# Keeping the second part of every mix, cross and up weight tile in DRAM after the first pass

## The chip, the cores and the metric

The kernel runs on one core of a Trainium2 chip. The metric is device time in microseconds of one execution. Three runs of the kernel before gave 1808.7, 1804.29 and 1805.51 us, a median of 1805.51. The profiled execution took 1804.14 us; its trace spans 1802.0 us, so 2.1 us lie outside the span.

## What is computed

One layer of an encoder runs over 1024 prompt frames and 32 sample frames with shared weights. The part that the change touches is the second half of the layer, cut to its core here:

```
bo = (cb * conv) @ w_conv_out
x  = x + (sigmoid(ga) * a + sigmoid(gb) * bo) @ w_mix_out
hc = rms_norm(x, g_cross)
cq = hc @ w_cq
s  = einsum(cq, mem_k) * MEM_SCALE ;  p = softmax(s)
x  = x + einsum(p, mem_v) @ w_co
hm = rms_norm(x, g_mlp)
x  = x + square(relu(hm @ w_up)) @ w_down
```

The model width is 1024, the hidden width 4096, the cross-attention has 4 heads of 64 over 256 memory tokens. All inputs and outputs are float32.

## The kernel before

**Two parts for each operand.** Each matrix product is made of three TensorE products in a rounded float32 format. A helper, `split`, makes the two parts of an operand: ScalarE copies the value into the rounded format (`hi`), and VectorE subtracts `hi` from the value (`lo`). `gemm` then adds up, for each block of 128 rows, `hi*hi`, `hi*lo` and `lo*hi` (lines 183, 184 and 185), the last one with the weight's `lo` tile, which the code calls `wl`.

**The weight stream.** A weight tile has 128 partitions of 1024 numbers (512 KB). The list `worder` holds the tiles in the order of their use, and `next_w` keeps two tiles ahead of the one in use (`LOOK = 2`). `issue_w` prepares one tile: SyncE's queue loads the raw tile into one of two `wr` buffers (line 145), ScalarE casts it into one of three `wh` buffers and VectorE subtracts into one of three `wl` buffers (lines 125 and 126 inside `split`). A raw buffer is free again when both have read it. A `wh` or `wl` buffer is free when the products with the tile three places earlier are done.

**Three passes over the same weights.** The frames are cut into three chunks of 384, 384 and 288 columns (chunks 0, 1 and 2; the last one holds the sample frames too). The products with `w_conv_out` (8 tiles), `w_mix` (8), `w_cq` (2), `w_co` (2) and the first 8 tiles of `w_up` are made chunk by chunk, so each of these tiles is prepared three times. One tile then serves one product of 24 matmuls.

**Kept second parts.** The dictionary `kept` names tiles whose `wl` is stored in DRAM when it is first made (line 162, right behind the subtraction). In the passes for the chunks 1 and 2 such a tile's `wl` is loaded (line 156), and ScalarE alone casts `wh` (line 157). Before the change `kept` holds the tiles with odd numbers: 4 of `w_conv_out`, 4 of `w_mix`, 1 of `w_cq`, 1 of `w_co` and 4 of the first 8 of `w_up`, 14 in all, hence 14 stores and 28 loads.

**The order around them.** `trunk(c)` is the list of conv_out products and mix products of chunk c. `do_conv_out` loads a partial result (line 1026), `do_mix` loads a slice of x (line 1041), adds it to the product (line 1045), and forms two parts of the scaled sum for the cross-attention (lines 262 and 263). `cross_steps(c)` is the cross-attention of chunk c: query products, scores, turns, values (lines 1156 to 1171) and the output product `do_co` (lines 1183 to 1185, its sum at 1187). `beside` interleaves the cross steps of a chunk with the products of the next one: cross 0 beside trunk 1, cross 1 beside trunk 2, cross 2 beside the up products of the chunks 0 and 1. `normed_split` (lines 1212 to 1216) prepares the MLP's input of the chunks 0 and 1. After these come the up products of chunk 2, together with `combine` (lines 1261 to 1273), which prepares sums and differences for the later up tiles, and then those tiles themselves.

**What decides the order of instructions.** The code gives a program order; a scheduler moves instructions within each engine's stream by its own estimates of time, except those inside `pin`. Each engine runs its stream in order. All DMAs named here, loads, stores and weights, are issued on SyncE's queue in its stream order: one that waits for its data or its buffer holds back all behind it. Product sums lie in three PSUM banks (`acc`); a bank is free when VectorE has read it.

Of the kernel before, what the change touches and what calls it, by code (L numbers as in the profile page):

```python
# [10 lines left out]
F32 = mybir.dt.float32  # L11
# [27 lines left out]
def hybrid_step(ctx: ExitStack, tc: tile.TileContext, io):  # L39
    nc = tc.nc  # L40
    act, dve, pool_e, pe, sp = nc.scalar, nc.vector, nc.gpsimd, nc.tensor, nc.sync
# [3 lines left out]
    def nm(s):  # L45
        uid[0] += 1
        return f"{s}_{uid[0]}"
# [64 lines left out]
    plan, worder, kept = [], [], {}  # L112
# [11 lines left out]
    def split(hi, lo, src):  # L124
        act.copy(hi, src)  # L125
        dve.tensor_sub(lo, src, hi.bitcast(F32))  # L126
# [15 lines left out]
    def fetch_w():  # L142
        raw = wp.tile([P, 1024], F32, tag="wr", bufs=2, name=nm("wr"))
        src = weight(worder[wpos[0] + len(fetched)])
        sp.dma_start(raw.rearrange("p (i c) -> p i c", i=4) if len(src.shape) == 3 else raw, src)
        fetched.append(raw)

    def issue_w():
        if not fetched:
            fetch_w()  # L150
        raw = fetched.pop(0)
        key = worder[wpos[0]]
        hi = wp.tile([P, 1024], F32R, tag="wh", name=nm("wh"))
        lo = wp.tile([P, 1024], F32R, tag="wl", name=nm("wl"))
        if kept.get(key) is not None:
            sp.dma_start(lo.bitcast(F32), kept[key])
            act.copy(hi, raw)
        else:
            split(hi, lo, raw)
            if key in kept:  # L160
                kept[key] = dram.tile([P, 1024], F32, name=nm("wl_d"))
                sp.dma_start(kept[key], lo.bitcast(F32))
        ready.append((worder[wpos[0]], (hi, lo)))
        wpos[0] += 1

    def next_w(key):
        while len(ready) <= LOOK and wpos[0] < len(worder) and worder[wpos[0]] is not STOP:
            issue_w()
        k, w = ready.pop(0)
        assert k == key, (k, key)  # L170
        return w
# [106 lines left out]
    def norm_x():  # L278
# [37 lines left out]
        with tc.manual_schedule(engines={mybir.EngineType.Activation, mybir.EngineType.DVE}):  # L316
            parts(0, range(2))
            issue_w()
            parts(0, range(2, NF))
            issue_w()  # L320
            issue_w()
            squares(0)
# [115 lines left out]
    def do_K(pr, extras=()):  # L438
        def fn(w):
            kt = at_tile([P, NT], F32, "kt")  # L440
            ktt[pr] = kt
            for c, (o, n) in enumerate(CH):
                a = acc_tile([P, n])
                gemm(a, w, xg[c])
                dve.tensor_mul(kt[:, o : o + n], a, R[c])
                after(extras, c)
            sp.dma_start(io["o_k"][pr], kt[:, 896:])

        return fn
# [22 lines left out]
    def do_Q(kv, j, extras=()):  # L472
        def fn(w):
            for c, (o, n) in enumerate(CH):
                npr = min(n, NPR - o)
                if j == 0:
                    qs[kv, c] = at_tile([P, 4, npr], F32R, "QA" if c < 2 else "QB", 2 if c < 2 else 1)
                    if n > npr:
                        qs[kv, 3] = at_tile([P, 4, n - npr], F32R, "QC")
                a = acc_tile([P, n])  # L480
                gemm(a, w, xg[c])
                t = tmp(n)
                dve.scalar_tensor_tensor(t, a, 0.125, R[c], op0=ALU.mult, op1=ALU.mult)
                parts = [(qs[kv, c], slice(0, npr))]
                if n > npr:
                    parts.append((qs[kv, 3], slice(npr, n)))
                for q, s in parts:
                    for e in range(2):
                        own, other = slice(64 * e, 64 * e + 64), slice(64 - 64 * e, 128 - 64 * e)
                        h = 2 * j + e  # L490
                        act.copy(q[own, h], t[own, s])
                        dve.tensor_sub(q[other, h], t[own, s], q[own, h].bitcast(F32))
                after(extras, c)

        return fn
# [156 lines left out]
    def do_gate(to, extras=()):  # L652
        def fn(w):
            for c, (o, n) in enumerate(CH):
                a = acc_tile([P, n])
                gemm(a, w, xg[c])
                t = gate_slot(c, 0)
                dve.tensor_mul(t, a, R[c])
                act.activation(t, t, AF.Sigmoid)
                to(c, t)  # L660
                after(extras, c)

        return fn
# [59 lines left out]
    for i, h in enumerate(hosts):  # L723
# [16 lines left out]
        if h[0] == "Q":  # L740
            fn, key = do_Q(h[1], h[2], extras), qt(h[1], h[2])
        elif h[0] == "K":
            fn, key = do_K(h[1], extras), ("w_in", 8 + h[1])
        elif h[0] == "G":
            fn, key = do_gate(lambda c, t: sa.__setitem__((c, 0), t), extras), ("w_in", 34)
        else:
            fn, key = do_conv(*h, extras), conv_w(h[1], h[0])
# [743 lines left out]

    up0 = lambda c: [do_up(j, c) for j in range(NF)]
    for name, n in (("w_conv_out", NF), ("w_mix", NF), ("w_cq", 2), ("w_co", 2), ("w_up", NF)):
        kept.update(((name, j), None) for j in range(1, n, 2))

    left = beside([], trunk(0), [(i, lambda: pump(2)) for i in range(NF)])
    item(lambda: pump(0))
# [343 lines left out]
```

## Time and profile before

| | |
|---|---|
| runs | 1808.7, 1804.29, 1805.51 us (median 1805.51) |
| profiled execution | 1804.14 us |
| its span in the trace | 1802.0 us |
| mean granted TensorE clock | 0.991 |
| DVE busy over the span | 1172.4 us (65%) |
| ACT busy over the span | 797.2 us (44%) |
| HBM read and written | 242.62 MB and 86.67 MB |
| stores of `wl` (line 162) | 14, from 802.5 to 1092.4 us |
| loads of `wl` (line 156) | 28, from 869.2 to 1173.3 us |

In the rows of the trace, PE is TensorE's matmuls, PEld its weight loads, DVE is VectorE, ACT ScalarE, POOL GpSimd and SP SyncE, whose DMA queue is SPq. L126 is line 126 of the kernel. In a view of windows, each engine has its busy time in the stretch and its number of instructions, then come the clock that TensorE was granted, the busy share of the 16 DMA engines and the GB/s that they moved. In a view of waits, a row names who waited, for whom, the total in us, the number of times and the longest. In a timeline, a row has start and duration in us, engine, line, operation and tiles; a bracket holds the idle time ahead of it and what ended it. Matmuls are pipelined, so their rows overlap; the distance of the starts is what one costs.

### The profile page before, as it was taken

The numbers are of one execution on the slowest core, as the hardware profiler recorded it, in microseconds if no ns is written. First come the engines' busy times: TensorE is split into PE (matmuls) and PEld (weight loads), VectorE is DVE, ScalarE is ACT, GpSimd is POOL, SyncE is SP. The second block draws the span as 40 slices with busy tenths as digits, with TensorE's granted clock in tenths as the row PEclk, the third lists the DMA queues.
The fourth block names the chain that finished last, engine by engine and source line by source line (L and its number), as shares of the span: only waits on it lengthen the run. The fifth ranks groups of instructions, "written<-read, shape, count | busy, mean of one in ns | idle before, by whom it ended". The sixth has DMA issues, their size and how long they took to land. (4 is left out here: it accounts for less than half of the span.)

```text
span 1802.0 us, 30258 instructions
## 1 busy us (share of the span) xinstructions
PE 1756.7 (97%) x11110; PEld 1736.2 (96%) x11110; DVE 1172.4 (65%) x2164; ACT 797.2 (44%) x1566; POOL 593.8 (33%) x681
## 2 busy tenths in 40 slices
PE   8999999999999999999999999999999899999998
PEld 7999999999999999999999989999999899999997
DVE  6776767868665646647566867776666566436673
ACT  8643535435344334335565745632222334324453
POOL 0013245653454444502224242385555300100101
PEclk9999999999999999999999989999999999999999
DMA  5332234344346888758755656744433577436573
GB/s 180 100 112 92 87 109 147 118 151 143 127 150 237 308 288 276 262 200 274 256 194 205 231 204 233 260 151 152 141 122 131 172 243 240 161 126 205 195 248 125
DMA packets 184002, 331.27 MB, mean 184 GB/s; under 512 B 18784, under 2 KB 139648, under 8 KB 183728
## 3 DMA queue, kind: packets, MB, share of 16 engines
q1 hardware_dynamic: 170080, 280.95, 46.6%
q0 software_dynamic: 13776, 48.41, 7.6%
q8 instruction: 87, 1.43, 0.3%
q14 instruction: 59, 0.48, 0.1%
HBM read 242.62 MB, written 86.67 MB: 183 GB/s over the span
## 5 line engine op out<-in xcount | busy, mean ns | idle before, releaser
L125 ACT CAST wh<-wr 128x1024 fp32r<-128x1024 f32 x224 | 235.3, 1050 | 405.4 <-PE acc L184 106.2
L126 DVE TENSOR_TENSOR wl<-wr,wh 128x1024 fp32r<-128x1024 f32 x224 | 298.0, 1330 | 169.8 <-ACT wh L125 158.4
L183 PE MATMUL acc<-X,wh 128*128 128x384 f32 (+1 forms) x864 | 282.1, 327 | 8.4 <-ACT wh L125 8.4
L184 PE MATMUL acc<-X,wh 128*128 128x384 f32 (+1 forms) x864 | 279.4, 323 | 0.0
L185 PE MATMUL acc<-X,wl 128*128 128x384 f32 (+1 forms) x864 | 278.7, 323 | 0.2 <-DVE wl L126 0.2
L183 PE MATMUL acc<-Y,wh 128*128 128x384 f32 (+1 forms) x624 | 202.2, 325 | 3.7 <-ACT Y L762 2.2
L184 PE MATMUL acc<-Y,wh 128*128 128x384 f32 (+1 forms) x624 | 201.7, 324 | 0.3 <-DVE Y L763 0.3
L185 PE MATMUL acc<-Y,wl 128*128 128x384 f32 (+1 forms) x624 | 201.8, 324 | 0.0
L259 POOL TENSOR_TENSOR xacc<-xacc,ct 128x384 f32<-128x384 f32 (+1 forms) x62 | 74.7, 1206 | 339.3 <-ACT ct L257 337.5
L183 PEld LDWEIGHTS acc<-X,wh 128*128 128x128 f32 x864 | 163.0, 189 | 9.0 <-ACT wh L125 8.4
L184 PEld LDWEIGHTS acc<-X,wh 128*128 128x128 f32 x864 | 163.4, 189 | 0.6
L185 PEld LDWEIGHTS acc<-X,wl 128*128 128x128 f32 x864 | 163.1, 189 | 0.8 <-DVE wl L126 0.8
L183 PEld LDWEIGHTS acc<-Y,wh 128*128 128x128 f32 x624 | 117.4, 189 | 5.1 <-ACT Y L762 2.8
L184 PEld LDWEIGHTS acc<-Y,wh 128*128 128x128 f32 x624 | 117.5, 188 | 0.9 <-DVE Y L763 0.9
L185 PEld LDWEIGHTS acc<-Y,wl 128*128 128x128 f32 x624 | 117.5, 189 | 0.0
L1587 PE MATMUL acc<-Y,wh 128*128 128x384 f32 (+1 forms) x352 | 113.6, 323 | 0.7 <-DVE lt L1378 0.7
L1588 PE MATMUL acc<-Y,wh 128*128 128x384 f32 (+1 forms) x352 | 113.6, 323 | 0.0
L1589 PE MATMUL acc<-Y,wl 128*128 128x384 f32 (+1 forms) x352 | 113.3, 322 | 0.0
L125 ACT CAST PTh<-pt 128x512 fp32r<-128x512 f32 (+3 forms) x94 | 46.2, 517 | 116.4 <-PE pt L572 108.2
L851 PE MATMUL acc<-Y,wh 128*128 128x384 f32 x248 | 84.0, 339 | 1.7 <-ACT s L1335 0.9
L707 POOL TENSOR_TENSOR ws<-ws 128x256 f32<-128x256 f32 x92 | 82.8, 899 | 5.2
L1244 POOL TENSOR_TENSOR ct<-ct 128x288 f32<-128x288 f32 (+1 forms) x48 | 45.1, 941 | 119.0 <-DVE ct L1240 45.6
(360 smaller groups left out, 4767.8 us busy)
## 6 DMA issues: line engine op xcount, KB each, us to landing
wr<-in_w_in SPq DMA_DIRECT2D x52, 512.0 KB, 3.4
wr<-in_w_up SPq DMA_DIRECT2D x48, 512.0 KB, 3.8
wr<-in_w_down SPq DMA_DIRECT2D x32, 512.0 KB, 3.8
wr<-wsum_d SPq DMA_DIRECT2D x32, 512.0 KB, 3.6
wl<-wl_d SPq DMA_DIRECT2D x28, 512.0 KB, 4.2
wr<-in_w_conv_out SPq DMA_DIRECT2D x24, 512.0 KB, 4.5
wr<-in_w_mix SPq DMA_DIRECT2D x24, 512.0 KB, 4.3
ct<-b_d SPq DMA_DIRECT2D x48, 192.0 KB, 3.9
```

The costliest lines, as they stand in the source:

```text
L125: act.copy(hi, src)
L126: dve.tensor_sub(lo, src, hi.bitcast(F32))
L183: pe.matmul(out, wh[:, a], hi, start=(k == 0), stop=False)
L184: pe.matmul(out, wh[:, a], lo, start=False, stop=False)
L185: pe.matmul(out, wl[:, a], hi, start=False, stop=(k == len(acts) - 1))
L259: pool_e.tensor_tensor(acc, acc, sq, op=ALU.add)
L707: pin(pool_e.tensor_tensor(t[:, to], t[:, x], t[:, y], op=ALU.add))
L851: pe.matmul(acc, wh[:, a], hi, start=(start and k == 0), stop=False, skip_group_check=True)
L1244: pool_e.tensor_tensor(h, t, t, op=ALU.mult)
L1587: pe.matmul(a, wh[:, s], hi, start=(start and k == 0), stop=False, skip_group_check=True)
L1588: pe.matmul(a, wh[:, s], lo, start=False, stop=False, skip_group_check=True)
L1589: pe.matmul(a, wl[:, s], hi, start=False, stop=(stop and k == len(acts) - 1), skip_group_check=True)
```

## The change

Two things are changed. The store of a kept `wl` is no longer issued right behind its subtraction but is put on a list, `parts_out`, and issued at the beginning of the next `issue_w`. And `kept` holds all tiles of `w_mix`, `w_cq`, `w_co` and the first 8 of `w_up`, while of `w_conv_out` it holds the odd ones as before: 24 tiles, hence 24 stores and 48 loads.

```diff
+    parts_out = []
+
     def issue_w():
+        for to, lo in parts_out:
+            sp.dma_start(to, lo.bitcast(F32))
+        parts_out.clear()
         if not fetched:
             fetch_w()
         raw = fetched.pop(0)
@@
             split(hi, lo, raw)
             if key in kept:
                 kept[key] = dram.tile([P, 1024], F32, name=nm("wl_d"))
-                sp.dma_start(kept[key], lo.bitcast(F32))
+                parts_out.append((kept[key], lo))
         ready.append((worder[wpos[0]], (hi, lo)))
         wpos[0] += 1
@@
     for name, n in (("w_conv_out", NF), ("w_mix", NF), ("w_cq", 2), ("w_co", 2), ("w_up", NF)):
-        kept.update(((name, j), None) for j in range(1, n, 2))
+        kept.update(((name, j), None) for j in range(n) if j % 2 or name != "w_conv_out")
```

## The prediction

> **What bounds the kernel now.** I read the page first, then the stretch from 800 to 1190 us stage by stage, because all stores and loads of `wl` lie there (802.5 to 1173.3 us), then who TensorE waits for in it, and last the timelines around the waits.
>
> ```profile
> span 1802.0 us, 30258 instructions
> PE 1756.7 (97%) x11110; PEld 1736.2 (96%) x11110; DVE 1172.4 (65%) x2164; ACT 797.2 (44%) x1566; POOL 593.8 (33%) x681
> ...
> L126 DVE TENSOR_TENSOR wl<-wr,wh 128x1024 fp32r<-128x1024 f32 x224 | 298.0, 1330 | 169.8 <-ACT wh L125 158.4
> ```
>
> TensorE is the bound: 1802.0 - 1756.7 = 45.3 us idle in the whole kernel. The change adds and removes no matmul, so it can gain only idle TensorE time and time at a reduced clock. A subtraction of a weight tile takes 1.33 us of VectorE, which has 35% of the span to spare, so its busy time as such is worth nothing; only where it stands ahead of something that TensorE waits for does it count.
>
> ```profile
> core 0: us, PE busy (x) PEld busy (x) DVE busy (x) ACT busy (x) POOL busy (x), PEclk, DMA share, GB/s
> 800.00:880.00 80.00, 77.66 (x443) 76.24 (x442) 54.78 (x83) 42.16 (x72) 15.86 (x13) 1.00 0.82 280
> 880.00:960.00 80.00, 79.82 (x475) 79.12 (x474) 51.17 (x92) 46.44 (x88) 26.13 (x22) 1.00 0.60 203
> 960.00:1050.00 90.00, 83.36 (x552) 79.89 (x551) 64.73 (x125) 55.58 (x110) 27.94 (x28) 0.94 0.63 213
> 1050.00:1140.00 90.00, 87.81 (x553) 86.45 (x552) 65.11 (x125) 49.41 (x105) 22.54 (x22) 1.00 0.65 223
> 1140.00:1190.00 50.00, 46.98 (x329) 46.12 (x328) 39.43 (x56) 27.81 (x47) 34.53 (x29) 1.00 0.79 275
> ```
>
> The rows are, from the top: trunk 0; cross 0 beside trunk 1; cross 1 beside trunk 2; cross 2 beside the up products of the chunks 0 and 1; the up products of chunk 2. TensorE's idle time in them is 2.3, 0.2, 6.6, 2.2 and 3.0 us, 14.4 in all. The third row holds almost half of it, has the busiest VectorE of the first four and is the only one with a clock below 1.00.
>
> ```profile
> PE acc L1183 <- DVE Gb L1045: 2.8, 3, 1.5
> PE acc L1183 <- DVE Ga L1187: 1.5, 3, 0.9
> PE acc L1183 <- ACT Y L1165: 1.3, 2, 0.9
> PE acc L183 <- DVE ct L1240: 1.3, 1, 1.3
> PE o L1156 <- DVE tO L1159: 1.2, 1, 1.2
> ```
>
> These are TensorE's five longest waits from 860 to 1190 us. Four of them are for VectorE; none is for a load of `wl`, though 28 of them stand in the stretch.
>
> **What the removed subtractions are worth.** The change removes 20 subtractions, 2 for each of the 10 newly kept tiles, 20 x 1.33 = 26.6 us of VectorE. The comparison of the two instruction orders agrees: VectorE has 20 rows fewer (1955 to 1935). Three of the removed ones stand at stalls.
>
> ```profile
> 1026.49 1.21 DVE L126 TENSOR_TENSOR wl<-wr,wh 128x1024 fp32r<-128x1024 f32 x1
> ...
> 1028.09 0.54 DVE L1159 TENSOR_TENSOR tO<-o,tO 64x384 f32<-64x384 f32 x1
> ...
> 1030.79 1.21 DVE L126 TENSOR_TENSOR wl<-wr,wh 128x1024 fp32r<-128x1024 f32 x1
> ...
> 1033.90 0.44 DVE L1045 TENSOR_TENSOR Gb<-acc,ct 128x288 f32<-128x288 f32 x1
> ```
>
> ```profile
> 1028.68 0.45 PE L1156 MATMUL o<-PTh,mv 128*128 128x384 f32 x1 [1.15 <-DVE tO L1159]
> ...
> 1034.39 0.45 PE L1183 MATMUL acc<-Y,wh 128*128 128x384 f32 x1 [1.45 <-DVE Gb L1045]
> 1034.68 0.34 PE L1184 MATMUL acc<-Y,wh 128*128 128x384 f32 x1
> 1034.85 0.33 PE L1185 MATMUL acc<-Y,wl 128*128 128x384 f32 x1
> 1035.59 0.44 PE L1183 MATMUL acc<-Y,wh 128*128 128x384 f32 x1 [0.40 <-ACT Y L1165]
> 1036.71 0.44 PE L1184 MATMUL acc<-Y,wh 128*128 128x384 f32 x1 [0.68 <-DVE Y L1171]
> ...
> 1038.26 0.69 PE L1183 MATMUL acc<-Y,wh 128*128 128x384 f32 x1 [0.93 <-DVE Ga L1187]
> 1038.74 0.52 PE L1184 MATMUL acc<-Y,wh 128*128 128x384 f32 x1
> 1039.06 0.52 PE L1185 MATMUL acc<-Y,wl 128*128 128x384 f32 x1
> ```
>
> VectorE runs without a gap from the first subtraction to the add at 1033.90. The sum at 1028.09, which ends TensorE's wait of 1.15 us, comes 1.2 us earlier without it; the add that ends the wait of 1.45 us comes up to 2.4 us earlier without both. In the changed kernel's order neither stands there any more. Both waits go: 2.6 us. The later waits (0.40, 0.68, 0.93) are turns between ScalarE, VectorE and TensorE on the last head; I leave them in.
>
> **The clock.** Starts of neighbouring matmuls are 0.17 us apart at 1034.68 and 0.32 us apart at 1038.74.
>
> ```profile
> 1038.00:1048.00 10.00, 8.38 (x26) 7.37 (x27) 6.86 (x13) 5.08 (x10) 4.88 (x6) 0.51 0.32 98
> ```
>
> Just behind the series of waits the granted clock falls to 0.51 for 10 us. TensorE is busy for 8.38 us of it, so about 8.38 x 0.49 = 4.1 us are lost. The series from 1027.5 to 1038.3 holds 1.15 + 1.45 + 0.40 + 0.68 + 0.93 = 4.6 us of idle time; without the first two 2.0 are left. I take it that the clock then stays up, and count 4.1 us; the bounds are 0 and 4.1.
>
> The Trainium skill's page "TensorE: Matmul & The Clock Gate", section "What's actually happening", says that the clock falls to half after at least one idle window of about 3.4 us. No single wait here is longer than 1.45 us, so by that sentence the waits would not be the cause, removing two of them would not bring the clock back, and the sum would lack this term. The trace has the fall right behind them, and I go by the trace.
>
> **The stall in chunk 2's up products.**
>
> ```profile
> 1161.34 1.05 ACT L125 CAST wh<-wr 128x1024 fp32r<-128x1024 f32 x1 [3.18 <-DMA wr<-in_w_up]
> 1162.42 1.23 DVE L126 TENSOR_TENSOR wl<-wr,wh 128x1024 fp32r<-128x1024 f32 x1 [3.92 <-ACT wh L125]
> 1163.56 0.45 DVE L1240 SCALAR_TENSOR_TENSOR ct<-acc,R 128x288 f32<-128x288 f32 x1
> 1164.06 0.40 PE L183 MATMUL acc<-Y,wh 128*128 128x288 f32 x1 [1.27 <-DVE ct L1240]
> 1164.30 0.29 PE L184 MATMUL acc<-Y,wh 128*128 128x288 f32 x1
> 1164.43 0.30 PE L185 MATMUL acc<-Y,wl 128*128 128x288 f32 x1
> ```
>
> Here VectorE's stream stood for 3.92 us at a subtraction whose raw tile came late, and the eviction behind it, which frees TensorE's bank, had to wait though it needed neither. The subtraction of this tile (an even one of `w_up`) is removed: 1.3 us gained, the late raw tile being then ScalarE's matter alone.
>
> **What is added.** 10 stores and 20 loads of 512 KB, 15.7 MB, all on SP's queue.
>
> ```profile
> L156 SPq DMA_DIRECT2D wl<-wl_d x28: 319/326/656, 869.2 to 1173.3; - x28
> ...
> DMA to landing us min/median/max: 3.5/4.2/6.0
> ```
>
> ```profile
> SPq L156 <- PE acc L185: 34.3, 18, 4.0
> ```
>
> A load waits on SP until the products of the tile three places earlier have freed its buffer, and SP stands meanwhile for 34.3 / 18 = 1.9 us on the mean. Behind it are the slices of x (line 1041), the stores of normed rows and the raw tiles. From the freed buffer, two products are left until the tile is needed: 2 x 24 matmuls at 0.17 us in the chunks 0 and 1, 8.2 us, and at 0.13 us in chunk 2 (the starts at 1164.30 and 1164.43), 6.2 us. The median load is there after 0.33 + 4.2 = 4.5 us, the slowest after 6.3. All 28 loads of before cost TensorE nothing, so I count the 20 new ones at 0; the bounds are 0 and the second rival's price below.
>
> The stores of `w_mix` fall into the first stage, which runs at 280 GB/s and 0.82 of the DMA engines. There the 4 new ones add 2.1 MB, 26 GB/s over 80 us, and the share goes to about 0.90. Weight tiles are short there at one place:
>
> ```profile
> PE acc L183 <- ACT wh L125: 1.6, 1, 1.6
> ```
>
> I count this wait once more, 1.6 us; the bounds are 0 and once for each of the 4 stores, 6.4 us. The other 6 stores (2 of cross weights, 4 of `w_up`) go where the share is 0.60 to 0.65 and I count them at 0. That a store is issued one tile late changes next to nothing: in both orders it stands just ahead of the raw load of the tile two places on, and both wait for the same subtraction. Its cover is that shared wait; without it a store would cost SP its 0.33 us of issue.
>
> **The sum.** -2.6 - 4.1 - 1.3 + 1.6 = -6.4 us. Against the profiled execution that is 1804.1 - 6.4 = 1797.7. That execution lies 1.4 us below the median of the runs shown, so for a run I say 1799.
>
> **The rivals.**
>
> *The clock falls all the same.* The remaining waits of 2.0 us within 4 us, or a new order around them, could bring it down again. For this speaks that 0.93 us of them directly precede the slow matmul at 1038.26. Then the sum is -2.3 and the time about 1803. It is also the result by the page's sentence on the idle window.
>
> *The loads of `wl` land late* (slower). The place is the up products, from 1100 to 1185 us, where in both passes every tile now needs one.
>
> ```profile
> 1140.00:1150.00 10.00, 10.00 (x64) 9.83 (x63) 7.85 (x14) 7.52 (x16) 5.41 (x6) 1.00 0.98 372
> ```
>
> The DMA engines are already full there for 10 us, and 4 more loads fall into the last stage alone. The mechanism decides from the point where a load takes over 6.2 us from freed buffer to landing. If it takes twice the median, 0.33 + 8.4 = 8.7 us, two tiles need 8.7 instead of 6.2, 1.25 us more a tile, 10 us over 8 tiles. With the gains above but for the stall at 1164, which would then only move, that is 1805.5 - 2.6 - 4.1 + 1.6 + 10 = 1810. Against it: the slowest of 28 loads took 6.0 us.
>
> *More than the three stalls goes.* If all idle time from 960 to 1050 us went as well as the slow clock, it would be 6.6 + 4.1 + 1.3 - 1.6 = 10.4 us, 1795. Against it: part of that waiting is for slices of x, which now stand behind more waiting loads on SP.
>
> ```profile
> DVE Gb L1045 <- DMA ct<-in_x: 5.2, 2, 3.1
> ```
>
> *The change does not do what it says.* The instruction order shows the 20 subtractions gone and the 30 DMAs there, so I give this nothing.
>
> **How the numbers follow.** The forecast has 0.42, its own range 1797 to 1802; the clock that falls all the same 0.27, 1800 to 1806; late loads 0.21, 1806 to 1816; more than the stalls 0.10, 1792 to 1797. A change of under 0.3%, 5.4 us, cannot be told from none by runs that spread over 4.4 us; so faster means below 1800.1, slower above 1810.9. Below 1800.1 lie most of the forecast (0.33), the last case (0.10) and a little of the second (0.02): 0.45. Above 1810.9 I put three quarters of the late loads, 0.16, and 0.04 for places that I have not priced: 0.20. The rest, 0.35, is within. The range 1793 to 1812 leaves out the far ends of the two outer cases.
>
> **What would show it.** In the profile after: no wait over 0.5 us for lines 1159 and 1045 near 1030 us, a clock of 1.00 from 1030 to 1050 us, and no stall at the first evictions of chunk 2's up products. Wrong would be a granted clock near 0.5 in that stage as before, waits of line 185 for a DMA `wl<-wl_d`, landings above 6.2 us there, or longer waits for weight casts in the mix products of chunk 0.

## The result and the profile after

The changed kernel takes 1811.64 us (median of 21 runs, 1807.22 to 1814.47), the kernel before in the same comparison 1805.5 us (21 runs). The ratio is 1.0032, 95% interval 1.0023 to 1.0041: 0.32% or about 6 us slower, where 6.4 us less were forecast. The profiled execution is a short one, 1807.3 us with a span of 1805.5 us; two more executions of the same kernel that were traced later have spans of 1808.4 and 1807.6 us. The trace shown is therefore read for where time goes, and the medians for how much it is.

The head of the page after, and the row of the weight subtractions in its costliest groups:

```profile
span 1805.5 us, 30279 instructions
...
PE 1756.0 (97%) x11110; PEld 1736.4 (96%) x11110; DVE 1143.3 (63%) x2144; ACT 796.3 (44%) x1566; POOL 574.9 (32%) x681
...
L126 DVE TENSOR_TENSOR wl<-wr,wh 128x1024 fp32r<-128x1024 f32 x204 | 268.3, 1316 | 153.2 <-ACT wh L125 152.5
```

The 20 subtractions are gone and VectorE is busy for 29 us less, yet TensorE's idle time has risen from 45.3 to 49.5 us (1805.5 - 1756.0). The five stages, in the view of windows (span of the window, busy time and instructions of PE, PEld, DVE, ACT and POOL, granted clock, DMA share, GB/s):

```profile
800.00:880.00 80.00, 77.09 (x430) 75.52 (x429) 51.66 (x78) 39.69 (x69) 14.90 (x13) 0.98 0.86 294
880.00:960.00 80.00, 80.00 (x479) 79.89 (x478) 50.73 (x93) 47.61 (x91) 23.48 (x22) 1.00 0.74 246
960.00:1050.00 90.00, 79.88 (x539) 76.98 (x538) 53.52 (x115) 53.81 (x105) 21.49 (x24) 0.97 0.72 247
1050.00:1140.00 90.00, 89.11 (x560) 88.75 (x559) 57.36 (x120) 50.35 (x108) 25.95 (x25) 0.99 0.81 275
1140.00:1190.00 50.00, 47.40 (x322) 46.38 (x321) 31.04 (x53) 27.22 (x47) 28.48 (x29) 0.97 0.93 337
```

TensorE's idle time, before and after: 2.3 and 2.9; 0.2 and 0.0; 6.6 and 10.1; 2.2 and 0.9; 3.0 and 2.6 us. The time that the clock costs (PE busy times one less the granted clock) has to be added. It is 5.0 us in the third row before and 0 in the others; after, it is 1.5, 0, 2.4, 0.9 and 1.4 us. Both together rose by 2.1, -0.2, 0.9, -0.4 and 1.0 us, which makes 3.4 of the 3.5 us between the two spans. So in these two traces the first and the last row lose as much as the third; what belongs to the change and what to the single execution, the runs below have to tell.

Idle time alone rose most in the third row. VectorE lost 11 us of work there (64.7 to 53.5), and TensorE idles 3.5 us more. That speaks against VectorE's load of work as what TensorE waits for there. The longest waits of TensorE from 860 to 1190 us (who waited, for whom: total us, times, longest):

```profile
PE acc L188 <- DVE Ga L1050: 4.5, 2, 2.7
PE acc L1188 <- DVE Gb L1050: 4.0, 3, 2.6
PE acc L188 <- ACT wh L162: 1.8, 1, 1.8
PE acc L1188 <- DVE Ga L1192: 1.6, 1, 1.6
PE acc L190 <- DMA wl<-wl_d: 0.7, 1, 0.7
```

The wait for `tO` (1.2 us before) is gone. In first place stand two rows for line 1050, the add of x to the mix product, which was line 1045 and cost 2.8 us before. What VectorE itself waits for, from 1000 to 1060 us:

```profile
DVE Gb L1050 <- DMA ct<-in_x: 3.5, 2, 2.7
DVE Ga L1050 <- DMA ct<-in_x: 3.5, 2, 2.9
```

The adds wait for their slices of x. That is not new: before, VectorE waited for slices of x for 6.3 us in this window (5.2 for `Gb`, 1.1 for `Ga`). What is new is that TensorE waits with it, 8.5 us in place of 2.8. One of the adds, on VectorE and then on TensorE (a bracket holds the idle time ahead and what ended it):

```profile
1028.52 0.46 DVE L1050 TENSOR_TENSOR Ga<-acc,ct 128x288 f32<-128x288 f32 x1 [2.87 <-DMA ct<-in_x]
```

```profile
1029.03 0.40 PE L188 MATMUL acc<-M,wh 128*128 128x288 f32 x1 [1.80 <-DVE Ga L1050]
...
1035.98 0.40 PE L188 MATMUL acc<-M,wh 128*128 128x288 f32 x1 [2.67 <-DVE Ga L1050]
...
1046.82 0.69 PE L1188 MATMUL acc<-Y,wh 128*128 128x384 f32 x1 [2.56 <-DVE Gb L1050]
```

The slice was issued on SyncE's queue at 1020.60, 7.9 us ahead of the add:

```profile
1018.19 0.88 SPq L161 DMA_DIRECT2D wl<-wl_d  x2
1019.27 0.33 SPq L145 DMA_DIRECT2D wr<-in_w_mix  x1
1020.21 0.33 SPq L145 DMA_DIRECT2D wr<-in_w_co  x1
1020.60 0.45 SPq L1046 DMA_DIRECT2D ct<-in_x  x1
...
1023.85 0.38 SPq L161 DMA_DIRECT2D wl<-wl_d  x1
1027.99 0.33 SPq L145 DMA_DIRECT2D wr<-in_w_mix  x1
1028.42 0.38 SPq L161 DMA_DIRECT2D wl<-wl_d  x1
1029.28 0.33 SPq L145 DMA_DIRECT2D wr<-in_w_co  x1
1029.66 0.42 SPq L1046 DMA_DIRECT2D ct<-in_x  x1
```

Two `wl` tiles and two raw tiles, 2.1 MB, were issued in the 2.4 us ahead of a slice of 147 KB. At 372 GB/s, the rate of the fullest window quoted in the prediction, these take 5.6 us by this estimate. The next slice shows a second effect: it is issued only at 1029.66, behind four weight loads, the second of which started 4.1 us after the first (1023.85 and 1027.99). The landing times of the 8 slices of this pass, in the view of line 1046 from 1000 to 1060 us:

```profile
DMA to landing us min/median/max: 3.8/5.3/7.9
```

Before, in the view of line 1041:

```profile
DMA to landing us min/median/max: 3.2/3.8/5.5
```

From here two theories were tried against each other:

- *Slices of x.* The new loads of `wl` cost little by landing late themselves. They hold back the small loads of x behind them on SyncE's queue in the third pass, and the VectorE add of x then holds TensorE's bank.
- *Spread or other.* The loss comes from the stores, from the late store, from late `wl` tiles, or is spread over all stages as DMA traffic.

### The profile page after: what moved, and what is told of

It is laid out like the page before. It is cut to its first block, busy times and chain, and to the rows that moved or that the text cites. A ratio compares the mean times of both kernels' runs of the same rounds, so it can differ in the third digit from the quotient of the medians.

```text
span 1805.5 us, 30279 instructions
## 1 busy us (share of the span) xinstructions
PE 1756.0 (97%) x11110; PEld 1736.4 (96%) x11110; DVE 1143.3 (63%) x2144; ACT 796.3 (44%) x1566; POOL 574.9 (32%) x681
## 5 line engine op out<-in xcount | busy, mean ns | idle before, releaser
L125 ACT CAST wh<-wr 128x1024 fp32r<-128x1024 f32 x204 | 214.2, 1050 | 386.2 <-PE acc L189 82.5
L126 DVE TENSOR_TENSOR wl<-wr,wh 128x1024 fp32r<-128x1024 f32 x204 | 268.3, 1316 | 153.2 <-ACT wh L125 152.5
L264 POOL TENSOR_TENSOR xacc<-xacc,ct 128x384 f32<-128x384 f32 (+1 forms) x62 | 70.4, 1137 | 347.6 <-ACT ct L262 345.1
L857 PE MATMUL acc<-Y,wh 128*128 128x384 f32 x248 | 83.3, 336 | 0.0
L856 PE MATMUL acc<-Y,wh 128*128 128x384 f32 x248 | 83.2, 336 | 0.0
```

The lines of the kernel that those rows point to most:

```text
L264: pool_e.tensor_tensor(acc, acc, sq, op=ALU.add)
L856: pe.matmul(acc, wh[:, a], hi, start=(start and k == 0), stop=False, skip_group_check=True)
L857: pe.matmul(acc, wh[:, a], lo, start=False, stop=False, skip_group_check=True)
```

## The experiments

Each run was compared with the kernel before on the same chip. Ratios are to that kernel, with 95% intervals; the edits are against the changed kernel unless said otherwise.

### The parts of the change

**The late store alone.** The set of kept tiles is that of before.

```diff
-        kept.update(((name, j), None) for j in range(n) if j % 2 or name != "w_conv_out")
+        kept.update(((name, j), None) for j in range(1, n, 2))
```

> Only the first part of the change: the stores one tile late, the kept tiles as before. Its instructions stand in the same order as before on every engine, so it is a yardstick for the measurement: 1804 to 1806, ratio within 0.1% of one. If lateness itself mattered, it would move by more.

1803.99 us against 1803.38, ratio 0.9998 (0.9988 to 1.0009). The late store is worth nothing. As each engine has the same instruction order here as before, this trace is also a second trace of the kernel before.

**All stores, old loads.** All 24 tiles are stored, only the 14 odd ones are loaded; the other 10 are subtracted again.

```diff
-        if kept.get(key) is not None:
+        if kept.get(key) is not None and key[1] % 2:
...
-            if key in kept:
+            if key in kept and kept[key] is None:
```

> The changed kernel with all 24 second parts stored, but only the 14 odd ones loaded in the later passes; the other 10 are subtracted again. Theory A (the stores of w_mix delay the loads of the memory values and the weights in the first mix products, the 2.7 us lost by 860 us): about 2 to 3 us slower than before, 1808, with a stall of about 2 us near 852 us. Theory B (the 20 new loads make the loss by holding back and slowing the loads of x): as before, 1805 to 1806.

1803.45 us against 1804.5, ratio 0.9992 (0.998 to 1.0005). The 10 added stores cost nothing that can be measured; the interval reaches from 3.6 us faster to 0.9 us slower. The loss needs the loads.

**Families.** The condition in the last line of the diff decides which weights keep all tiles; the other ones keep their odd tiles.

```diff
-... if j % 2 or name != "w_conv_out")
+... if j % 2 or name == "w_mix")                          (mix only)
+... if j % 2 or name in ("w_cq", "w_co", "w_up"))         (cross and up)
+... if j % 2 or name not in ("w_conv_out", "w_co"))       (all but co)
+... if j % 2 or name not in ("w_conv_out", "w_up"))       (all but up)
```

> All 8 tiles of w_mix kept, of the others the odd ones. If the mix products carry the loss (stores in the first pass, loads of x behind weight loads in the third), it is nearly all of it: +4 to +5 us, 1810. If the up products carry it, +0 to +1 us, 1806.

> All tiles of w_cq, w_co and the first 8 of w_up kept, of w_mix and w_conv_out the odd ones. If the mix products carry the loss: 0 to +1 us, 1806, and the gain of the two subtractions of w_co near 1027 us may show (-1 to -3 us, 1803). If late loads in the up products carry it: +4 to +6 us, 1810.

> The changed kernel with w_co back at its odd tile. The theory that the third pass loses because each of its tiles, mix and co, now brings a raw and a second-part load in a row: without the co tile between the mix tiles the burst is half a MB shorter, x is less late, and about half of the 6 us is back, 1807 to 1809. If the up products carry the rest: 1811.

> The changed kernel with w_up back at its odd tiles. If the third pass of the mix products carries the loss, it stays at +5 to +6 us, 1810 to 1811. If late loads in the up products carry it, it falls to +1 us, 1806.

| all tiles kept of | median us | ratio (95%) |
|---|---|---|
| mix | 1806.41 | 1.0008 (0.9996 to 1.0019) |
| cq, co, up | 1803.43 | 0.9990 (0.9980 to 1.0001) |
| mix, cq, up | 1803.57 | 0.9989 (0.9978 to 0.9999) |
| mix, cq, co | 1806.69 | 1.0005 (0.9995 to 1.0016) |
| mix, cq, co, up (the change) | 1811.64 | 1.0032 (1.0023 to 1.0041) |

The families do not add up: mix alone and the rest alone give 1.0008 and 0.9990, together 1.0032. Something is used up only when they are together. One tile of `w_co` (the even one, with two loads) makes the difference from 0.9989 to 1.0032, where half of the loss was expected back, and the first of its loads, for chunk 1, falls into the stage of the third pass. A cost by number of loads or bytes would not look like this; a queue in one stage that mix and co tiles share would. Two of the four runs came out the other way: by what was written down before them, mix alone at 1.0008 and all but up at 1.0005 speak for the up products as the place. These runs are also not clean, as the scheduler orders the instructions anew for each set: in the trace of all but co, the order on VectorE differs from the changed kernel's at several places between 1030 and 1051 us. How much of a ratio is order and how much is loads, they do not tell.

### The queue of the x slices

**All 24 slices on ScalarE's queue**, in the changed kernel and, as a control, in the kernel before.

```diff
-            sp.dma_start(xt, io[f"x{c}"][:, f])
+            act.dma_start(xt, io[f"x{c}"][:, f])
```

> The changed kernel with the loads of x for the mix products issued on ScalarE's queue instead of SP's, all else in the same order. Theory B1 (x is late because it stands behind waiting loads and 0.5 MB transfers on SP's queue): the waits of the add of x in the third pass, 7 us in the changed kernel, shrink to under 2 us and the time falls by 3 to 6 us, to 1806 to 1809. Theory B2 (the DMA engines as a whole are short): x lands as late as before and the time stays at 1811 to 1812.

> Control: the kernel before with the loads of x for the mix products on ScalarE's queue. If those loads are late only because of the added second-part loads, this is as before, 1803 to 1806; if they were as costly before, it is 4 to 6 us faster, 1799 to 1801, and the 5 us that this edit won on the changed kernel say nothing of the change.

The changed kernel falls to 1803.64 us, ratio 1.0002 (0.9988 to 1.0015). That is more than was expected, though VectorE's waits for x in the third pass fell only to 3.3 us, not under 2. In the traces of this edit and the next two, VectorE, ScalarE and GpSimd have the changed kernel's instructions in the changed kernel's order, so here the queue alone is changed. The control takes 1804.22 against 1805.3, 0.9989 (0.9979 to 1.0): of the 0.30% that the edit is worth in the changed kernel, some 0.11% are also to be had in the kernel before, with an interval that just reaches zero. The rest, about 0.19%, belongs to the change.

**Only the 8 slices of the third pass, and only the other 16.**

```diff
-            sp.dma_start(xt, io[f"x{c}"][:, f])
+            (act if c == 2 else sp).dma_start(xt, io[f"x{c}"][:, f])     (third pass)
+            (sp if c == 2 else act).dma_start(xt, io[f"x{c}"][:, f])     (the other two)
```

> The changed kernel, with only the 8 slices of x of chunk 2 (third pass, 1000 to 1060 us) loaded from ScalarE's queue; the other 16 stay on SyncE's. If the loss comes from those slices being late behind the weight loads in the third pass, nearly all of the recovery seen with all 24 slices is there: ratio 0.999 to 1.0010, TensorE idle from 1015 to 1060 us down from 8 to 10 us to about 6. If the loss is spread over the stages and the 24 slices each gave a little: 1.0015 to 1.0030.

> The complement: the 16 slices of x of the chunks 0 and 1 from ScalarE's queue, the 8 of chunk 2 left on SyncE's. Third-pass theory: the loss stays, 1.0025 to 1.0040, and TensorE is idle for 8 to 10 us from 1015 to 1060 us. Spread theory: 1.0005 to 1.0020. A ratio near 1.000 would say that the lateness in the chunk-0 mix products (852 us) is what costs.

Third pass: 1805.1 us against 1803.97, ratio 1.0010 (0.9999 to 1.0021). The other 16 slices: 1809.72 us, ratio 1.0035 (1.0022 to 1.0049), the whole loss. That places the larger part: 8 slices of 147 KB on another queue take back 0.22% against the changed kernel and 0.25% against the run with the other 16, 4 to 4.5 us, and 16 slices take back nothing. In the trace of the third-pass edit, the landing of these slices from 1000 to 1060 us and TensorE's waits from 1015 to 1060 us are

```profile
DMA to landing us min/median/max: 2.1/3.9/6.4
```

```profile
PE acc L188 <- DVE Ga L1050: 3.0, 2, 2.1
PE acc L1188 <- DVE Ga L1192: 2.0, 1, 2.0
PE acc L1188 <- DVE Gb L1050: 0.8, 2, 0.5
```

TensorE waits 3.8 us for the adds of line 1050 in place of 8.5 (6.7 and 6.4 in the changed kernel's other two traces). Most adds still start as their slices land; the slices land earlier. A single trace is a rough tool, though: the complement's trace, which was expected to show 8 to 10 us of idle time from 1015 to 1060 us, shows 45 - 38.35 = 6.65 us, no more than the third-pass edit's 6.7, and only 4.5 us of waits for line 1050. It lost its time by the clock instead. Over the window from 1000 to 1065 us, idle time (65 less PE busy) and the time lost to the clock (PE busy times one less the granted clock) read as follows:

| trace | PE busy | clock | idle | lost to the clock | sum |
|---|---|---|---|---|---|
| before | 58.31 | 0.92 | 6.7 | 4.7 | 11.4 |
| late store only | 57.26 | 0.95 | 7.7 | 2.9 | 10.6 |
| changed | 54.64 | 0.95 | 10.4 | 2.7 | 13.1 |
| changed, second trace | 55.76 | 0.89 | 9.2 | 6.1 | 15.4 |
| changed, third trace | 56.84 | 0.95 | 8.2 | 2.8 | 11.0 |
| x of the first two passes moved | 58.11 | 0.89 | 6.9 | 6.4 | 13.3 |
| x of the third pass moved | 58.06 | 0.97 | 6.9 | 1.7 | 8.7 |
| all of x moved | 59.55 | 0.95 | 5.5 | 3.0 | 8.4 |
| all but co | 58.36 | 0.97 | 6.6 | 1.8 | 8.4 |

The four traces with the change's loads and its slices on SyncE's queue have 11.0 to 15.4 us, 13.2 on the mean, the two of before 10.6 and 11.4, and the three where the slices of the third pass are moved or one `w_co` tile is left out 8.4 to 8.7. On the mean, then, the third pass without the delayed slices is 2 to 3 us better than before, the size of the two waits that the prediction saw go; with them it is some 2 us worse.

The two further traces of the changed kernel come from these runs:

> The changed kernel once more beside the others, for a second trace. If its loss belongs to its instructions, it is again 5 to 6 us slower than before (ratio 1.003) and the trace shows the late loads of x in the third pass again. If the loss was of the chips or moments of the first runs, the ratio is within 0.1% of one.

> A third trace of the changed kernel, to tell what is the same in all of them (waits for loads of x and for weights) from what comes and goes (the granted clock in single windows). The third pass from 1015 to 1060 us is again 2 us or more behind the kernel before at equal progress.

1809.71 us against 1803.38, ratio 1.0035 (1.0023 to 1.0047), and 1809.69 us in a single run.

**The same work in every trace.** A window of fixed times holds a little more or less of the program in each trace; between the same two instructions the work is the same. The table has the time from the last multiplication of line 1035 (the last conv_out product) to the last add of line 1050, which is the third pass of mix products, and from that add to the last subtraction of line 1374, which lies in the later up tiles. In the kernel before and its control these are the lines 1030, 1045 and 1369.

| trace | third pass, us | behind it, us |
|---|---|---|
| before | 50.7 | 380.0 |
| late store only | 50.8 | 380.6 |
| before, all of x moved | 51.0 | 378.3 |
| all stores, old loads | 49.2 | 378.7 |
| mix only | 49.0 | 379.2 |
| all but up | 49.5 | 379.5 |
| changed, three traces | 52.1, 53.8, 49.7 | 380.8, 381.2, 381.0 |
| x of the first two passes moved | 51.4 | 382.1 |
| x of the third pass moved | 48.5 | 380.4 |
| all of x moved | 48.0 | 381.8 |
| all but co | 48.9 | 381.2 |
| cross and up | 47.5 | 382.9 |
| cross and up, x moved (below) | 46.7 | 381.3 |
| `wl` on GpSimd's queue (below) | 52.0 | 381.4 |

In the third pass, the four traces with the change's loads and slices on SyncE's queue take 51.7 us on the mean, the four with the old loads 50.4, and the two with the slices moved 48.5 and 48.0. This agrees with the table above. But the changed kernel's third trace is at 49.7 us no slower than before, where 2 us or more behind was expected: single executions differ by as much as the effect, and it is the medians that carry it.

The last column shows a second place. The six traces that load `wl` only for the odd tiles of `w_up` take 378.3 to 380.6 us, 379.4 on the mean; the nine that load it for all of them on SyncE's queue take 380.4 to 382.9, 381.4 on the mean. Moving the slices of x changes nothing here. From 1060 to 1445 us TensorE waits in each of the nine for a cast of line 162 (1.4 to 3.7 us) and for a load of `wl` (0.5 to 1.7 us), and in none of the six. This place rests on traces and on the run with all but up; no run moves a queue there to test it.

### Other queues

**`wl` on GpSimd's queue**, so that neither x nor raw tiles stand behind a waiting `wl` load.

```diff
-            sp.dma_start(lo.bitcast(F32), kept[key])
+            pool_e.dma_start(lo.bitcast(F32), kept[key])
```

> The changed kernel with the loads of wl issued on GpSimd's queue, so that SP neither waits for TensorE nor carries these 0.5 MB transfers, x staying on SP. Theory B1 (x is held back on SP's queue by them): x is in time again, the third pass loses under 1 us against before, total 1804 to 1808, unless GpSimd, now waiting for TensorE, delays its own sums. Theory B2 (the DMA engines are short, wherever a transfer is issued): 1811 to 1812.

1809.75 us, ratio 1.0020 (1.0005 to 1.0035). This doesn't tell the theories apart. VectorE's waits for x in the third pass fell to 1.8 us, as the theory has it, but TensorE still waits 3.3 us there for line 1050, and 4.8 us in place of 1.6 for the sums of line 1192. GpSimd's stream now stands 81.3 us, in 28 waits, at loads whose buffer TensorE has not freed, and its own work stands behind.

**The best set with the better queue**: cross and up tiles only, and all of x on ScalarE's queue.

> All of w_cq, w_co and w_up kept, w_mix at its odd tiles, and the loads of x on ScalarE's queue: the two edits that came out below one so far. If their gains (0.1% each) are real and independent, 0.2% faster than before, 1801 to 1802; if both are noise, 1804 to 1806.

1802.58 us against 1803.38, ratio 0.9987 (0.9976 to 0.9999). It is the lowest ratio of all runs, but its interval hardly differs from that of cross and up tiles without the edit (0.9990), or of all but co.

## Why the prediction failed, point by point

**The two waits, -2.6 us: right, but what was late next was not followed.** The `tO` wait of 1.2 us is gone. The add of line 1045 no longer stands behind two subtractions, but it still needs its slice of x, and that now arrives after the point where the subtractions would have let it run. The prediction knew it: it names slices of x "behind more waiting loads on SP" as the argument against its best case, and prices it nowhere. It should have asked when each slice on TensorE's path would land with the loads in front of it counted. With the slices moved, the third pass is about 2 us faster than before (48.5 and 48.0 us against 50.4), so the gain was there to be had.

**The 20 loads, counted at 0: the step that failed.** The reason given was that "All 28 loads of before cost TensorE nothing", which is about the loads' own landings. On that point the forecast was nearly right: the 48 loads have

```profile
DMA to landing us min/median/max: 3.4/4.8/8.9
```

instead of 3.5/4.2/6.0, and TensorE's products wait 0.7 us for one of them. But the price of a load is also what it does to the other loads. By the moved slices it is 4 to 4.5 us in the third pass; of moving all 24 slices, the kernel before would gain 2 us as well (the control's 0.11%), so a part may not be the change's. In the up products and behind them it is another 2 us or so, by the traces. The view that showed the danger was quoted: SyncE stood 34.3 us, 18 times, at such loads. After, it is

```profile
SPq L161 <- PE acc L190: 66.7, 31, 4.7
```

The slower rival, late `wl` loads in the up products from 1100 to 1185 us, had the right sign, the right objects and one of the two places, at 2 us or so in place of the 10 that it priced. Its mechanism, a product that waits for its own `wl`, is there with 0.7 us; the larger wait there is for a raw tile's cast. It did not see the slices of the third pass. All four signs that the prediction named for being wrong are there: a clock near 0.5 in the third pass, a wait for a `wl` load, landings of `wl` up to 8.9 us from 1100 to 1185 us, and the longer wait for weight casts in chunk 0's mix products.

**The clock, -4.1 us: did not come.** In the changed kernel the clock falls again, a little later: in windows of 4 us,

```profile
1040.00:1044.00 4.00, 2.38 (x12) 2.01 (x12) 2.61 (x4) 1.80 (x4) 1.46 (x2) 1.00 0.74 252
1044.00:1048.00 4.00, 1.45 (x6) 1.19 (x5) 1.56 (x4) 0.54 (x1) 1.08 (x2) 0.65 0.37 133
1048.00:1052.00 4.00, 4.00 (x15) 4.00 (x14) 2.90 (x5) 1.77 (x3) 2.26 (x3) 0.50 0.16 53
```

The rival "the clock falls all the same" was right on this. Beyond it, the table shows that 4.1 us was partly an accident of one trace: the same instruction order loses 4.7 us in one execution and 2.9 in another, the changed kernel 2.7, 6.1 and 2.8. A clock term read from one trace has that spread, and the sum treated it as a fixed debt to be repaid.

**The stall in chunk 2's up products, -1.3 us: gone, and replaced by a longer one.** The first eviction no longer waits. But some 14 us later TensorE waits 1.8 us for the cast of another tile, and before that 0.7 us for a `wl` tile. ScalarE had stood for a late raw tile, then had the casts of `combine` to do, and came late to this one:

```profile
1173.62 1.06 ACT L162 CAST wh<-wr 128x1024 fp32r<-128x1024 f32 x1 [4.12 <-DMA wr<-in_w_up]
...
1176.88 1.04 ACT L162 CAST wh<-wr 128x1024 fp32r<-128x1024 f32 x1
1177.97 0.40 PE L188 MATMUL acc<-Y,wh 128*128 128x288 f32 x1 [1.81 <-ACT wh L162]
```

The raw loads themselves land later. In the view of line 145 from 1150 to 1190 us, before and after:

```profile
DMA to landing us min/median/max: 3.9/5.0/6.9
DMA to landing us min/median/max: 4.3/6.4/7.3
```

The idle time from 1140 to 1190 us fell by 0.4 us, but 1.4 us are now lost to the clock there, and none were before. The prediction said that the late raw tile would be "ScalarE's matter alone"; ScalarE's cast is what the product needs.

**The stores of mix, +1.6 us: the size about right, the path not shown.** In chunk 0's mix products, TensorE's wait is longer:

```profile
PE acc L188 <- ACT wh L125: 2.2, 2, 1.9
```

It was 1.6 us. The cast of `wh` stands on ScalarE behind a cast of memory values, which waits for its load:

```profile
851.17 0.40 ACT L1073 CAST mv<-mvr 128x256 fp32r<-128x256 f32 x1 [2.40 <-DMA mvr<-mv_d]
851.49 1.99 ACT L125 CAST wh<-wr 128x1024 fp32r<-128x1024 f32 x2
```

On SyncE's queue that load was issued at 846.52, behind a `wl` store at 843.52 and three loads; before, it was at 845.25. The clock then costs another 27.17 x 0.06 = 1.6 us from 840 to 870 us. The run that stores all 24 tiles shows only 1.36 and 0.29 us of waits and a clock of 1.00 there. Up to the first load of a `wl`, at 871.9 us, it has the same matmuls and the same DMAs in the same order as the changed kernel, so this difference is one between two executions. From the first row of line 1035 to the 8th add of line 1050, idle time and clock cost 2.2 to 7.2 us in the eleven traces that store all mix tiles, 4.7 on the mean, and 2.3 to 3.6 us in the five that store the odd ones, 2.8 on the mean; nine of the eleven have a fall of the clock there, and none of the five. A cost of about 2 us is likely by these traces, but the median of the run with all stores does not show it.

**What stays open.** Leaving out only the up tiles also recovers 0.27%, about 5 us. In its trace the stretch behind the third pass is 1.8 us shorter than in the traces with the change's loads, where the waits for the cast and the `wl` tile are gone, and the third pass is 2.2 us shorter, though most up tiles are prepared after it; the latter is not explained. Nor is it settled why the third-pass edit stays at 1.0010 while all of x moved gives 1.0002; the intervals overlap.

## What to carry to other kernels

A load that costs its consumer nothing can still be expensive: list what stands behind it on its queue, and look for the smallest transfer there that something on the critical path waits for. When a wait is removed, work out when each of the other inputs of the waiting instruction will be there, with the change's own transfers counted, before booking the wait as a gain. A fall of the clock seen in one trace is worth its mean over several, not its size in that one. And to find where the time went, add what the clock costs to the idle time, and compare between the same two instructions rather than the same two times.

## What the runs showed of the hardware

**The clock falls in steps that depend on more than the length of the stall.** After the 1.95 us wait that ends at 852.65 us, the changed kernel's windows of 1 us are

```profile
853.00:854.00 1.00, 0.72 (x4) 0.30 (x2) 1.00 (x1) 1.00 (x3) 0.00 (x0) 1.00 0.70 205
854.00:855.00 1.00, 0.99 (x4) 0.84 (x4) 1.00 (x2) 1.00 (x3) 0.10 (x1) 0.54 0.42 152
855.00:856.00 1.00, 1.00 (x5) 1.00 (x4) 1.00 (x2) 0.63 (x2) 1.00 (x1) 0.50 1.09 406
856.00:857.00 1.00, 1.00 (x5) 1.00 (x4) 1.00 (x3) 0.00 (x0) 0.10 (x1) 0.50 1.00 229
857.00:858.00 1.00, 1.00 (x6) 1.00 (x5) 1.00 (x3) 0.98 (x2) 0.00 (x0) 0.76 1.00 225
```

The clock is halved for 0.46 / 0.5 + 2 + 0.24 / 0.5 = 3.4 us, with TensorE busy, and 1.7 us are lost. The trace of the late store alone has a longer wait at the same place,

```profile
853.49 0.45 PE L188 MATMUL acc<-M,wh 128*128 128x384 f32 x1 [2.12 <-ACT wh L125]
```

and its clock is 1.00 from 848 to 858 us. The Trainium skill, page "TensorE: Matmul & The Clock Gate", section "What's actually happening", says that activity is watched in free-running windows of about 3.4 us. A step of 3.4 us agrees with that, and so does a longer wait at the same place without a fall; that a whole idle window is needed does not, as the longest wait ahead of this fall is 1.95 us, and in the third pass 2.7 us.

**The queue matters for small transfers.** The Trainium skill, page "DMA: Bandwidth & Descriptors", section "Issuing engines are not separate DMA queues", says that issuing from several engines only saves the time to issue. Here 8 loads of 147 KB had a median landing of 5.3 us on SyncE's queue (4.8 us in the run that moves only the other 16) and 3.9 us on ScalarE's, in a kernel whose other transfers stayed the same, and the kernel was 0.22% faster. Whether the packets pass the large loads or are only issued at a better moment these runs do not tell apart.
